# A hybrid decoder step: layer 0's input brought in row-major and channel-major, with no transposes

## The chip, the cores and the metric

The kernel runs on one core of a Trainium2 chip. The core has five engines that run side by side and meet at semaphores: TensorE (matrix products, written to PSUM), VectorE, ScalarE, GpSimd and SyncE, which here only issues DMAs. The metric is the device time of one execution in microseconds; a kernel's time is the median of its runs.

## The reference

One inference step of a decoder of two layers. Each layer adds to the residual `h` what four mixers (HGRN2, gated DeltaNet, Mamba-2 SSD, retention) make of one input projection of the normed residual:

```python
def rms_norm(x, w):                      # over the 1024 channels of a row
    x = x * lax.rsqrt(jnp.mean(x * x, axis=-1, keepdims=True) + EPS)
    return x * w
...
for l in range(DEPTH):                   # DEPTH = 2
    dp, sp = mixer(rms_norm(hp, norm_w[l]), pos_p, *lw, *zero_states(bsz), True)
    hp = hp + dp                         # prompt: 16 meta tokens + 2048 tokens, 1024 channels
    ds, ss = mixer(rms_norm(hs, norm_w[l]), pos_s, *lw, *past, False)
    hs = hs + ds                         # 8 sample tokens
```

Inside `mixer`, `proj = hn @ w_in_l` has 1024 x 4108 weights. Everything is float32.

## The kernel before

**Tiles and blocks.** The tokens are 17 tiles: tile 0 holds 16 empty rows, the 16 meta tokens and the 8 sample tokens (40 rows), tiles 1 to 16 hold 128 prompt tokens each. They form eight blocks of two tiles, the first of three. For each layer the kernel goes over all blocks in passes, one per mixer: C (SSD), B (DeltaNet), A (HGRN2), D (retention), then the output projection. The weights of a pass stay in SBUF while the blocks go by.

**The normed input.** The dense products need the normed input with the channels on the partitions, as 8 groups of 128 channels by the tokens, and split in two float32r parts: `xh` (rounded) and `xl` (the rest); three products `xh·wh`, `xl·wh`, `xh·wl` make one of nearly float32 accuracy (L484 to L486 and L494 to L497). In layer 0, `prep0` (L1701) makes it in SBUF for a block and stores it to DRAM too (L1708); passes B, A and D load it from there (`load_x`, L474). `prep0` calls `xprep` (L507) with `keep`. For a tile, `xprep` works on the token rows `hx`: ScalarE sums the squares (L358), GpSimd makes the power -1/2 (L340, L336), VectorE scales rows by it and by the norm weights, which lie in `sq128` spread over all partitions, in two halves of 512 channels (L514); TensorE transposes eight squares of 128 x 128 into two PSUM banks (L519); ScalarE rounds each bank into `xh` (L524), VectorE subtracts into `xl` (L525). In layer 1 the input comes from the output projection and goes through the same `xprep` without `keep`.

**Order.** In pass C of layer 0 `nextx(blocks[b.i + 1])` stands ahead of `mixC(L, W, b)`: the input of the next block is prepared while this block is computed. A planner orders the instructions of each engine by program order, with priorities, against a simulated timeline; engines run their lists in order. At the start the first block's input, the eight weight pieces of pass C (`wpiece`, L438: load, ScalarE's rounding L458, GpSimd's subtraction L459) and the constants come in together. Row tiles, weight pieces and some others share the pool `f4`: five buffers of 128 x 1024 float32 (L222). TensorE's dense results go to two PSUM banks (`pd`), transposes and small products to two others (`tr`). Nearly all DMAs are issued by SyncE's queue, in order.

Of the kernel before, what the change touches and what calls it, by code (L numbers as in the profile page):

```python
# [19 lines left out]
D = 1024  # L20
# [13 lines left out]
def make_consts(nch):  # L34
    f = np.float32
    jl = np.arange(32, dtype=f) * f(1 / 31)
    inv = (1 / (10000.0 ** jl.astype(np.float64)).astype(f)).astype(f)
    pos = np.zeros((nch + 1, 128), f)
    pos[0, 16:32] = np.arange(16)
    pos[0, 32:40] = PAST  # L40
    for c in range(nch):
        pos[c + 1] = 16 + 128 * c + np.arange(128)
    ang = (pos[:, :, None] * inv).astype(f).astype(np.float64)
    cs, sn = np.cos(ang).astype(f), np.sin(ang).astype(f)
    rope = np.concatenate([cs, sn], axis=-1).transpose(1, 0, 2).reshape(128, -1)
    g = np.log1p(-np.exp2(-5.0 - np.arange(4)))
    retdec = np.zeros((2, 128, 8), np.float64)
    for n, L in ((0, 32), (1, 128)):
        i = np.arange(L)[:, None]
        retdec[n, :L, :4] = np.exp(g * (i + 1))  # L50
        retdec[n, :L, 4:] = np.exp(g * (L - 1 - i)) / 8
    retdec[0, 32:40, :4] = 1
    retdec[0, 32:40, 4:] = 1 / 8
    p = np.arange(128)
    blk = p // 32
    i32 = np.arange(32)
    parts = {}
    j = (p % 32)[:, None]
    parts["hm0"] = j == i32
    parts["hm1"] = (j % 2 == 0) & (i32 == j + 1)  # L60
    for h in (2, 8):

        far = np.where(j // (4 * h) == i32 // (4 * h), i32 // h - j // h, 0)
        parts[f"hm{h}"] = np.concatenate([(far == d)[:, i32 // h % 4 >= d - (d == 1)] for d in (1, 2, 3)], axis=1)
    same = blk[:, None] == blk
    parts["l32s"] = same & (p[:, None] > p)
    parts["u32b"] = same & (p[:, None] <= p)
    parts["u32c"] = (p % 32)[:, None] <= i32
    parts["u128"] = p[:, None] <= p
    parts["hsame"] = (p // 64)[:, None] == p // 64  # L70
    rm = np.zeros((128, 4, 128))
    rm0 = np.zeros((128, 4, 32))
    for h in range(4):
        rm[:, h] = (p[:, None] <= p) * np.exp(-128 * g[h])
        rm0[:32, h] = (i32[:, None] <= i32) * np.exp(-32 * g[h])
    gg = np.stack([g[2 * pp + p // 64] for pp in range(2)], 1)
    parts["retgl"] = np.exp(128 * gg)
    parts["retg1"] = np.exp(gg)
    parts["retd0"] = retdec[0]
    parts["retd1"] = retdec[1]  # L80
    off, arrs, n = {}, [], 0
    for k, v in parts.items():
        off[k] = (n, n + v.shape[1])
        n += v.shape[1]
        arrs.append(v.astype(f))
    return rope[:, 64:], np.concatenate([rm.reshape(128, 512), rm0.reshape(128, 128), rope[:, 0:64],
                                           p[:, None] > p], axis=1).astype(f), np.concatenate(arrs, axis=1), off


class Seg:  # L90
# [3 lines left out]
def body(tc, ctx, a, o, nch, depth, blks, off):  # L94
# [268 lines left out]
    def load_layer(l):  # L363
        L = Seg()
        L.l = l
        for q in range(2):
            nc.sync.dma_start(sq128[q].rearrange("t h i -> t (h i)"),
                              a["norm_w"][l][512 * q:512 * q + 512].partition_broadcast(128))
        yield L
        pv = lp.tile([128, 10], F32, tag="pv", name="pv")  # L370
        for i, nm in enumerate(("hgrn_norm_w", "gdn_norm_w", "ssd_norm_w", "ret_norm_w", "ret_norm_b")):
# [132 lines left out]
            with early():  # L504
                evict(t, r)

    def xprep(L, t, hx, keep=False):  # L507

        b = next(x for x in blocks if t in x.tiles)
        R, x0 = rows(t), b.col[t]  # L510
        sc = rms_scale(hx, R)
        for q in range(2):
            hq = hx[0:R, 512 * q:512 * q + 512]
            stt(hq, hq, sc, sq128[q][0:R].rearrange("t h i -> t (h i)"), ALU.mult, ALU.mult)  # L514
        for q in range(2):
            ps = ptile(ptr, "tr")
            pv = ps.rearrange("p (d c) -> p d c", d=4)
            for d in range(4):
                T.transpose(pv[:, d, 0:R], hx[0:R, 512 * q + 128 * d:512 * q + 128 * d + 128], ident[0:R, 0:R])  # L519
            if keep:  # L520
                th, tl = (x[:, 4 * q:4 * q + 4, x0:x0 + R] for x in (b.xh, b.xl))
            else:
                th, tl = w2([128, 4, 128], "xth", F32R)[:, :, 0:R], w2([128, 4, 128], "xtl", F32R)[:, :, 0:R]
            S.copy(th, pv[:, :, 0:R])  # L524
            tt(tl, pv[:, :, 0:R], f32(th), ALU.subtract)  # L525
            for dst, src in () if keep else ((xhd, th), (xld, tl)):
                nc.sync.dma_start(f32(dst[b.i][:, 4 * q:4 * q + 4, x0:x0 + R]), f32(src))

    def silu2(ps, out, n):
# [1169 lines left out]


    def prep0(L, b):  # L1701
        b.xh, b.xl = xpair(b.i % 2, BW if b.i % 2 == 0 else 256)
        for t in b.tiles:
            hx = f4([128, D], "hx")
            load_h(0, t, hx)
            xprep(L, t, hx, True)
        for dst, src in ((xhd, b.xh), (xld, b.xl)):
            nc.sync.dma_start(f32(dst[b.i][:, :, :]), f32(src[:, :, 0:b.n]))  # L1708

# [115 lines left out]
def trace(nc, inputs):  # L1825
# [1 line left out]
    depth, nch = inputs["w_in"].shape[0], inputs["x_prompt"].shape[1] // 128  # L1827
    rope, retm, tab, off = make_consts(nch)
    arrays, a = {}, {}
    named = [(n, inputs[n]) for n in _INS] + [("c_rope", rope), ("c_retm", retm), ("c_tab", tab)]  # L1830
    for n, x in named:
        x = np.ascontiguousarray(x)
        arrays[f"in_{n}_dram"] = x
# [23 lines left out]
```

## Time and profile before

| | us |
|---|---|
| median of 3 runs | 2852.36 |
| lowest, highest | 2849.44, 2856.09 |
| the profiled execution | 2860.07 |
| its span in the trace | 2858.1 |
| TensorE busy in the span | 2702.7 |
| VectorE busy | 1712.1 |
| ScalarE busy | 1038.7 |
| GpSimd busy | 1066.1 |

The profile is one execution. PE is TensorE's products, PEld its weight loads, DVE is VectorE, ACT ScalarE, POOL GpSimd, SPq SyncE's queue. Products overlap in the pipeline, so that the time from one start to the next is shorter than the duration of one. In the rows, `L519 PE MATMUL tr<-ident,hx` is line 519, engine, operation, what is written and from what; `<-` behind a number names what ended an idle time.

### The profile page before, as it was taken

Reading aid. Unit: us, or ns where it says so; the run is one execution under the profiler, and the core shown is the slowest. Engines: PE = TensorE matmul, PEld = TensorE weight load, DVE = VectorE, ACT = ScalarE, POOL = GpSimd, SP = SyncE. Lnnn points to the kernel's source line nnn. Section 1 sums busy time; section 2 is a strip of 40 time slices with the busy share of each in tenths; the row PEclk is TensorE's granted clock in tenths of the full one; section 3 lists DMA queues with packets and bytes.
Section 4 is the critical chain, followed back from the end, with each engine's and each line's share of the span. In section 5 each row is a group of like instructions: output and inputs, shape, how many; then the busy total and the mean of one; then the engine's idle time right before and its main releaser. Section 6 shows DMA issues by size and latency. Waiting matters only on the chain.

```text
span 2858.1 us, 64542 instructions
## 1 busy us (share of the span) xinstructions
PE 2702.7 (95%) x25300; PEld 2461.8 (86%) x25300; DVE 1712.1 (60%) x4872; ACT 1038.7 (36%) x2621; POOL 1066.1 (37%) x2032
## 2 busy tenths in 40 slices
PE   6989999989999899999988999999999999999998
PEld 6889898889889789888878999989888887888887
DVE  5677765657656655464445767756676666445533
ACT  4445532333434422232243445223334443222321
POOL 4453546468323221210032535556673322212100
PEclk9999999999999999999999999999999999999999
DMA  7243455463321423236772423544632223331443
GB/s 177 69 139 106 148 136 146 130 175 103 108 74 61 149 77 113 77 99 212 224 227 80 127 104 115 154 121 140 181 106 72 76 89 109 99 102 67 145 140 111
DMA packets 385143, 349.16 MB, mean 122 GB/s; under 512 B 144312, under 2 KB 349616, under 8 KB 374600
## 3 DMA queue, kind: packets, MB, share of 16 engines
q1 hardware_dynamic: 381320, 335.95, 38.7%
q0 software_dynamic: 3520, 9.09, 1.6%
q8 instruction: 200, 3.28, 0.5%
q14 instruction: 103, 0.84, 0.1%
HBM read 247.05 MB, written 98.10 MB: 121 GB/s over the span
## 4 chain that ended last, share of the span: by engine, by line
PE 76%; DVE 8%; DMA 6%; ACT 3%; POOL 3%; issue 2%; SPq 1%; POOLq 0%; ACTq 0%; DVEq 0%
PE pd L494 10%; PE pd L495 9%; PE pd L497 9%; PE pd L484 9%; PE pd L485 9%; PE pd L486 9%; PE tr L236 7%; PE wo L236 4%; PE sc L236 4%; PE o L236 3%; DMA wr<-in_w_in_dram 3%; PE tr L623 1%; ACT wh L458 1%; PE tr L519 1%; DMA bld<-qkv 1%
## 5 line engine op out<-in xcount | busy, mean ns | idle before, releaser
L484 PE MATMUL pd<-xh,wh 128*128 128x256 f32 (+1 forms) x2816 | 826.9, 294 | 36.9 <-ACT wh L458 11.6
L485 PE MATMUL pd<-xl,wh 128*128 128x256 f32 (+1 forms) x2816 | 817.6, 290 | 0.0
L486 PE MATMUL pd<-xh,wl 128*128 128x256 f32 (+1 forms) x2816 | 813.2, 289 | 1.2 <-DVE wl L459 0.7
L484 PEld LDWEIGHTS pd<-xh,wh 128*128 128x128 f32 x2816 | 542.5, 193 | 58.1 <-issue 15.0
L494 PE MATMUL pd<-wh,xh 128*128 128x512 f32 (+5 forms) x1632 | 563.8, 346 | 8.1 <-DVE sraw L1409 5.1
L495 PE MATMUL pd<-wl,xh 128*128 128x512 f32 (+5 forms) x1632 | 560.0, 343 | 3.8 <-POOL wl L459 3.8
L485 PEld LDWEIGHTS pd<-xl,wh 128*128 128x128 f32 x2816 | 542.1, 193 | 5.5 <-issue 2.7
L486 PEld LDWEIGHTS pd<-xh,wl 128*128 128x128 f32 x2816 | 542.5, 193 | 4.5 <-issue 1.7
L497 PE MATMUL pd<-wh,xl 128*128 128x512 f32 (+4 forms) x1600 | 544.6, 340 | 0.0
L494 PEld LDWEIGHTS pd<-wh,xh 128*128 128x128 f32 (+1 forms) x1632 | 307.1, 188 | 44.8 <-issue 5.5
L495 PEld LDWEIGHTS pd<-wl,xh 128*128 128x128 f32 (+1 forms) x1632 | 307.4, 188 | 38.8 <-POOL wl L459 4.2
L497 PEld LDWEIGHTS pd<-wh,xl 128*128 128x128 f32 (+1 forms) x1600 | 299.8, 187 | 34.7 <-issue 2.0
L313 DVE TENSOR_TENSOR sbd<-low,tr 64x128 f32<-64x128 f32 x384 | 108.9, 284 | 122.0 <-PE tr L236 110.5
L336 POOL TENSOR_TENSOR fm<-fm,expo 128x4 f32<-128x4 f32 (+3 forms) x136 | 133.0, 978 | 85.4 <-DVE fm L614 78.0
L612 POOL TENSOR_SCALAR fm<-fm 128x4 f32<-128x4 f32 (+3 forms) x102 | 22.1, 216 | 363.2 <-DVE fm L609 335.8
L1683 DVE TENSOR_TENSOR hx<-hx,pd 128x512 f32<-128x512 f32 (+1 forms) x72 | 49.5, 687 | 153.1 <-PE pd L497 148.0
L340 POOL TENSOR_SCALAR rm<-rm 128x1 f32<-128x1 f32 (+1 forms) x51 | 14.1, 277 | 337.6 <-ACT junk L358 336.7
L244 POOL COPY bwi<-wz 32x256 f32<-32x256 f32 x128 | 58.7, 458 | 197.9 <-DVE wz L1267 195.6
L1171 POOL TENSOR_TENSOR bR<-bR,bW 128x120 f32<-128x120 f32 (+14 forms) x300 | 118.5, 395 | 20.3
L532 ACT ACTIVATE th<-pd 128x256 f32<-128x256 f32 (+2 forms) x162 | 62.6, 386 | 174.4 <-PE pd L486 130.3
L1170 POOL TENSOR_TENSOR bW<-bU,bR 128x120 f32<-128x120 f32 (+14 forms) x300 | 114.0, 380 | 29.8 <-DMA bR<-bscr 9.5
L458 ACT CAST wh<-wr 128x1024 fp32r<-128x1024 f32 x80 | 83.1, 1044 | 89.1 <-DMA wr<-in_w_in_dram 67.3
(524 smaller groups left out, 5055.7 us busy)
## 6 DMA issues: line engine op xcount, KB each, us to landing
xh<-xh SPq DMA_DIRECT2D x56, 1024.0 KB
xl<-xl SPq DMA_DIRECT2D x56, 1024.0 KB
wr<-in_w_in_dram SPq DMA_DIRECT2D x64, 512.0 KB
hx<-in_x_prompt_dram SPq DMA_DIRECT2D x32, 512.0 KB
y<-y SPq DMA_DIRECT2D x128, 128.0 KB
yf<-y SPq DMA_DIRECT2D x32, 512.0 KB
bld<-qkv SPq DMA_DIRECT2D x32, 384.0 KB
xh<-xh SPq DMA_DIRECT2D x8, 1184.0 KB
```

Of the source, the lines that this page charges most:

```text
L236: T.matmul(out, l, r, start=start, stop=stop, skip_group_check=True)
L313: tt(new[rr, :, hh], low[rr, :, hh], pv, ALU.add)
L336: G.tensor_tensor(dst, src, e.broadcast_to(list(src.shape)), ALU.pow)
L458: S.copy(hv[:, :, c0:c1], r)
L484: T.matmul(ps, hi[:, d], b.xh[:, d, 0:b.n], start=(d == 0), stop=False)
L485: T.matmul(ps, hi[:, d], b.xl[:, d, 0:b.n], start=False, stop=False)
L486: T.matmul(ps, lo[:, d], b.xh[:, d, 0:b.n], start=False, stop=(d == 7))
L494: T.matmul(ps[0:R, 0:n], xh[:, d], hi, start=(d == 0), stop=False)
L495: T.matmul(ps[0:R, 0:n], xh[:, d], lo, start=False, stop=xl is None and d == 7)
L497: T.matmul(ps[0:R, 0:n], xl[:, d], hi, start=False, stop=(d == 7))
L1170: f(wv, bcm(U_[0:2 * nu, j, j + 1:32], 1, m), bcl(R_[0:2 * nu, 0:m, j], 31 - j), ALU.mult)
L1171: f(R_[0:2 * nu, 0:m, j + 1:32], R_[0:2 * nu, 0:m, j + 1:32], wv, ALU.subtract)
```

## The change

Only layer 0 changes. The host hands in the same input a second time, as `c_xt`, with the channels on the partitions: for each tile 8 groups of 128 channels, side by side. `prep0` loads both forms of a tile, `hx` and `xt`, both from the pool `f4`. The rows serve only the sum of squares. One float32 product of the column `sc` (1/rms of each token, read 128 times over) with the identity puts the 1/rms of all tokens on every partition, in PSUM. VectorE then scales each of the eight channel groups in one operation by the norm weight, now a value per partition (`L.nw`, one load of 1024 single elements in place of the two broadcast loads of L367), and by that PSUM tile. ScalarE rounds all 1024 columns into `xh` at once, VectorE subtracts into `xl` at once, both from SBUF.

```diff
+def channel_major(inputs, nch):
+    f = np.float32
+    t0 = np.concatenate([np.zeros((16, D), f), inputs["meta_tokens"], inputs["x_sample"][:, 0]], axis=0)
+    tiles = [t0] + [inputs["x_prompt"][0, 128 * c:128 * c + 128] for c in range(nch)]
+    return np.concatenate([x.T.reshape(8, 128, len(x)).transpose(1, 0, 2).reshape(128, -1) for x in tiles], axis=1).astype(f)
...
-        for q in range(2):
-            nc.sync.dma_start(sq128[q].rearrange("t h i -> t (h i)"),
-                              a["norm_w"][l][512 * q:512 * q + 512].partition_broadcast(128))
+        if l == 0:
+            L.nw = lp.tile([128, 8], F32, tag="nw", name="nw")
+            nc.sync.dma_start(L.nw, a["norm_w"][l].rearrange("(d p) -> p d", p=128), allow_slow_non_contiguous=True)
+        else:
+            for q in range(2):
+                nc.sync.dma_start(sq128[q].rearrange("t h i -> t (h i)"),
+                                  a["norm_w"][l][512 * q:512 * q + 512].partition_broadcast(128))
...
         for t in b.tiles:
-            hx = f4([128, D], "hx")
+            R, x0 = rows(t), b.col[t]
+            hx, xt = f4([128, D], "hx"), f4([128, D], "hxt")
             load_h(0, t, hx)
-            xprep(L, t, hx, True)
+            o_ = 8 * (TR0 + 128 * (t - 1)) if t else 0
+            xt = xt[:, 0:8 * R]
+            nc.sync.dma_start(xt, a["c_xt"][:, o_:o_ + 8 * R])
+            sc = rms_scale(hx, R)
+            ps = ptile(ptr, "tr")
+            mm(ps[:, 0:R], sc.broadcast_to([R, 128]), ident[0:R, 0:R], True, True)
+            xv = xt.rearrange("p (d c) -> p d c", d=8)
+            for d in range(8):
+                stt(xv[:, d], xv[:, d], L.nw[:, d:d + 1], ps[:, 0:R], ALU.mult, ALU.mult)
+            th, tl = b.xh[:, :, x0:x0 + R], b.xl[:, :, x0:x0 + R]
+            S.copy(th, xv)
+            tt(tl, xv, f32(th), ALU.subtract)
```

`xprep` loses its argument `keep` and serves layer 1 alone.

## Rows read from the trace of the kernel before

**Rows 1.** The page: span, busy time by engine, chain that ended last
```profile
span 2858.1 us, 64542 instructions
...
PE 2702.7 (95%) x25300; PEld 2461.8 (86%) x25300; DVE 1712.1 (60%) x4872; ACT 1038.7 (36%) x2621; POOL 1066.1 (37%) x2032
...
PE 76%; DVE 8%; DMA 6%; ACT 3%; POOL 3%; issue 2%; SPq 1%; POOLq 0%; ACTq 0%; DVEq 0%
```

**Rows 2.** Stretches: us, busy PE PEld DVE ACT POOL, PEclk, DMA share, GB/s
```profile
0.00:40.00 40.00, 19.86 (x113) 18.30 (x114) 14.57 (x32) 16.79 (x27) 27.63 (x35) 0.96 0.89 222
40.00:330.00 290.00, 269.83 (x2099) 255.03 (x2098) 208.66 (x594) 152.48 (x384) 129.63 (x180) 0.97 0.39 119
```

**Rows 3.** Groups by shape, 0 to 330 us: | busy us, mean ns | idle before
```profile
L519 PE MATMUL tr<-ident,hx 128*128 128x128 f32 x128 | 21.7, 304 | 7.1 <-DVE xl L525 7.0
L525 DVE TENSOR_TENSOR xl<-tr,xh 128x512 fp32r<-128x512 f32 x32 | 21.7, 682 | 5.5 <-ACT xh L524 5.5
...
L958 DVE SCALAR_TENSOR_TENSOR cb<-pd,cwh,cb 128x256 f32<-128x256 f32 x42 | 20.0, 477 | 3.5 <-ACT cb L954 3.1
...
L524 ACT CAST xh<-tr 128x512 fp32r<-128x512 f32 x32 | 18.4, 583 | 15.8 <-PE tr L519 15.6
...
L458 ACT CAST wh<-wr 128x1024 fp32r<-128x1024 f32 x16 | 16.6, 1043 | 7.5 <-DMA wr<-in_w_in_dram 6.0 <-PE pd L485 1.4
...
L958 DVE SCALAR_TENSOR_TENSOR cb<-u,cwh,cb 128x32 f32<-128x32 f32 x6 | 1.5, 246 | 0.0
```

**Rows 4.** TensorE's weight loads in order of time: start, us
```profile
115.53 0.54 PEld L236 LDWEIGHTS tr<-cc,cb 128*128 128x128 f32 x4
...
219.44 1.01 PEld L519 LDWEIGHTS tr<-ident,hx 128*128 128x128 f32 x8
```

**Rows 5.** Lines 514 and 459, whole span: ns min/median/max
```profile
L514 DVE SCALAR_TENSOR_TENSOR hx<-hx,rm,sq x68: 734/747/2876, 9.1 to 1493.2; 128x512 f32<-128x512 f32 x64, 40x512 f32<-40x512 f32 x4
...
L459 DVE TENSOR_TENSOR wl<-wr,wh x40: 1200/1224/1505, 607.7 to 2659.2; 128x1024 fp32r<-128x1024 f32 x40
```

**Rows 6.** TensorE's waits, 40 to 330 us: total us, times, longest
```profile
PE sc L236 <- POOL cgu L1420: 8.4, 5, 4.3
PE tr L519 <- DVE xl L525: 3.2, 5, 1.1
...
PE pd L484 <- DVE hC L960: 2.0, 4, 0.8
...
PE tr L236 <- DVE xl L525: 0.8, 1, 0.8
```

**Rows 7.** The start-up in order of time, and DMA in 40 slices of 7.5 us
```profile
GB/s 183 308 107 175 400 184 174 67 53 109 243 3 3 9 9 279 20 20 4 3 280 20 35 263 114 263 214 130 32 227 182 20 19 73 74 331 34 20 87 361
...
26.51 1.34 SPq L451 DMA_DIRECT2D wr<-in_w_in_dram  x2
...
31.24 1.04 ACT L458 CAST wh<-wr 128x1024 fp32r<-128x1024 f32 x1 [2.41 <-DMA wr<-in_w_in_dram]
32.19 0.37 ACT L532 ACTIVATE th<-pd 40x256 f32<-40x256 f32 x1
...
33.24 0.56 PE L494 MATMUL pd<-wh,xh 128*128 128x268 f32 x1 [5.10 <-DVE sraw L1409]
```

**Rows 8.** The reader of a load of single elements
```profile
28.54 0.19 DVE L385 TENSOR_SCALAR cwh<-cwt 128x48 f32<-128x48 f32 x1 [3.65 <-DMA cwt<-in_ssd_conv_w_dram]
```

**Rows 9.** TensorE after a wait, and the granted clock of that stretch
```profile
160.00:190.00 30.00, 24.77 (x180) 22.96 (x179) 23.14 (x53) 13.18 (x33) 18.64 (x24) 0.89 0.46 131
...
182.00 0.80 PE L236 MATMUL sc<-cgu,l128r 128*128 128x512 f32 x1 [4.35 <-POOL cgu L1420]
...
186.30 0.43 PE L495 MATMUL pd<-wl,xh 128*128 128x268 f32 x1
...
186.71 0.28 PE L494 MATMUL pd<-wh,xh 128*128 128x268 f32 x1
```

More of the change, by code (lines that the diff above doesn't have):

```diff
@@ L505, in dense_tm, with xprep @@
                 evict(t, r)
-    def xprep(L, t, hx, keep=False):
+    def xprep(L, t, hx):
         b = next(x for x in blocks if t in x.tiles)
@@ L519, in xprep @@
                 T.transpose(pv[:, d, 0:R], hx[0:R, 512 * q + 128 * d:512 * q + 128 * d + 128], ident[0:R, 0:R])
[L520 to L523, printed above, removed]
+            th, tl = w2([128, 4, 128], "xth", F32R)[:, :, 0:R], w2([128, 4, 128], "xtl", F32R)[:, :, 0:R]
             S.copy(th, pv[:, :, 0:R])
             tt(tl, pv[:, :, 0:R], f32(th), ALU.subtract)
-            for dst, src in () if keep else ((xhd, th), (xld, tl)):
+            for dst, src in ((xhd, th), (xld, tl)):
                 nc.sync.dma_start(f32(dst[b.i][:, 4 * q:4 * q + 4, x0:x0 + R]), f32(src))
@@ L1829, in trace @@
     arrays, a = {}, {}
-    named = [(n, inputs[n]) for n in _INS] + [("c_rope", rope), ("c_retm", retm), ("c_tab", tab)]
+    named = [(n, inputs[n]) for n in _INS] + [("c_rope", rope), ("c_retm", retm), ("c_tab", tab),
+                                                ("c_xt", channel_major(inputs, nch))]
     for n, x in named:
```

## The prediction

> **What bounds the kernel now.** I read the page first, its busy shares and its chain of waits: TensorE is busy 95% of the span, and 76% of the chain that ended last is TensorE work, with VectorE next at 8% [rows 1]. So a microsecond counts if TensorE gets it back. The change touches only the first pass of layer 0 (mixer C over eight blocks, with the input preparation of the next block woven in), so next I cut that stage out by stretches. In the first 40 us TensorE is busy for half of the time: that is a start-up that waits for data. From 40 to 330 us it is busy 269.8 of 290 us (93%), VectorE 208.7 (72%), ScalarE 152.5 and GpSimd 129.6 [rows 2]. TensorE is the bound there and VectorE the runner-up. Then came the groups of the stage by shape, for prices [rows 3], the order of weight loads for TensorE's real cost [rows 4], and the list of what TensorE waited for between 40 and 330 us: mostly GpSimd's masked tiles (8.4 us), a little VectorE [rows 6]. The start-up I read last, engine by engine [rows 7].
>
> **What leaves TensorE.** 16 full tiles had eight transposes each, 128 in all [rows 3]. Eight of them run back to back in 1.01 us, 0.126 each [rows 4]. The first three tiles lie in the start-up, where TensorE is not the bound; I count tiles 3 to 16: 14 x 8 x 0.126 = 14.1 us. The replacement is one float32 product per tile, 128 x 128 by 128 columns, and the trace has such products in mixer C: they are issued as two halves each, and four halves take 0.54 us [rows 4], 0.27 a product, 14 x 0.27 = 3.8 us. Net: 10.3 us less on the engine that sets the end.
>
> **Waits that leave with them.** Transposes stopped for a PSUM bank that VectorE's subtraction still read: 3.2 us before L519, and 0.8 us before another matmul behind the same subtraction, from 40 us on [rows 6]. The new kernel takes one bank per tile instead of two, and its subtraction reads SBUF. I count 4.0 us gained; the bounds are 0 (the new product finds its bank held by eight small operations instead) and 4.0.
>
> **What VectorE gets.** Before, a tile cost two scalings of 128x512 and two subtractions of 128x512. I price the scalings at 0.75 us each (the median; a few take up to 2.88 [rows 5]) and the subtractions at 0.68 [rows 3]: 2.86 us. After: eight scalar-tensor-tensor operations of 128x128 with one operand in PSUM. The same operation takes 0.477 us at 256 elements and 0.246 at 32 [rows 3], so 0.00103 us an element and 0.213 fixed: 0.345 at 128, 2.76 for eight. The subtraction of 128x1024 from SBUF has its like in the weight split: 1.22 us [rows 5]. Sum 3.98, so 1.12 us more a tile, 14 x 1.12 = 15.7 us more of VectorE in a stage where it had 81 us free [rows 2]. Between nothing (it fills gaps) and all 15.7 I take a third, 5 us: it is nearer to nothing, since TensorE waited little for VectorE's evictions (2.0 us for the saved tail of the convolution, the next of its waits after the transposes') [rows 6], but VectorE would go from 72% to some 80%, and behind its eight operations in order stand the evictions that give TensorE its two dense banks back.
>
> Scaling in eight short pieces instead of two long ones is what the Trainium skill advises against: the page "VectorE: DVE Perf Modes", section "The TRN2 errata — SBUF-src ops pay a fixed extra latency per instruction", says that each instruction pays its latency once however short it is, and to keep tiles at 512 elements or more. Its formulas (58 cycles plus the elements for SBUF, 120 for PSUM, at 0.96 GHz) would make the eight pieces an estimated 2.07 us and the two 1.19; with that 0.74 us more a tile instead of 1.12, a third would be 3.5 us instead of 5, and the forecast 2844. The trace's fixed part, 0.213 us, is larger than the Trainium skill's 0.125, and the trace is what I use.
>
> **ScalarE, GpSimd, DMA.** ScalarE's two copies of 0.58 us from PSUM become one of 128x1024 from SBUF, which the weight split does in 1.04 us [rows 3]: 0.1 us less a tile, off the path, taken as nothing because VectorE's and TensorE's work covers it; if that cover went it would still be a gain. GpSimd's two operations a tile stay. SyncE's queue gets 17 more loads, 0.67 us of issue each if they cost what the two weight loads at 26.51 do [rows 7], some 11 us over 300, in a queue behind which stand the output stores and the stores of the prepared tiles, which nobody reads before the next pass. I cost them at nothing after the start; if a load has to wait for one of the five shared buffers, the stores behind it are late, and they have a pass of slack. The 8.4 MB over 300 us are 28 GB/s beside 119 at a DMA share of 0.39 [rows 2].
>
> **The start-up.** Here lies the larger uncertainty. The two broadcast loads of the norm weights (0.52 MB) go; one load in 1024 pieces of 4 bytes comes, and it is first in the queue. The nearest row is that of the convolution weights, several loads of 768 such pieces, whose reader at 28.54 waited 3.65 us for them [rows 8]. So some 4 to 6 us; the load is needed only after the first tile's load, sum of squares and power, and costs nothing by itself. The channel-major tiles of the first block are 1.21 MB more (296 rows of 4 KB). Net 0.69 MB more ahead of the weights, at 308 GB/s in the second 7.5 us [rows 7] 2.2 us. On the other side the row tile is free after the sum of squares instead of after its transposes, so weight pieces find a buffer sooner. Now TensorE stops for 5.10 us until 33.24: ScalarE has the eviction that would free its bank queued behind a weight piece that waits for its load, issued only at 26.51 when a buffer came free [rows 7]. Bounds: the stop goes (-5.1), or fourteen tiles instead of eleven in five buffers push the last two weight loads back by a tile's preparation each, (3.98 + 1.04) x 2 = +10. I take +2, the bytes.
>
> **The sum.** -10.3 - 4.0 + 5 + 2 = -7.3 us. The profiled execution took 2860.07 us (span 2858.1 and 2.0 around it [rows 1]); that makes 2852.8. The median of the runs shown, 2852.36, is 7.7 below the profiled one, so the forecast for a median is 2845.1, say 2845 (-0.26%). The runs of the kernel before scatter by 0.1% to either side, and 0.2% (5.7 us) is about what can be told from no change.
>
> **Rivals.** (1) VectorE swallows the gain. If about 12 of its 15.7 us reach TensorE: -10.3 - 4.0 + 12 + 2 = -0.3, 2852. For it: 72% busy, in order, two dense banks only; against it: the short waits for VectorE in [rows 6]. (2) VectorE becomes late and the clock makes it worse; this one ends slower. A wait of 4.35 us at 182 us is followed by 268-column matmuls of 0.43 us, where 0.28 is normal, until about 186.5: 4.5 us at the lower of the two clock levels, half of which is lost; the granted clock over 160 to 190 is 0.89 [rows 9]. So a wait can cost half as much again. All 15.7 us on the path, with that, are 23.6: -14.3 + 23.6 + 2 = +11, 2863. It decides once VectorE costs TensorE more than 18.0 us (14.3 - 2 + 5.7). [...] (3) The start-up starves: +10 instead of +2 gives +0.7, 2853. For it: five shared buffers; against it: the earlier release of row tiles. (4) The start-up gains as well: the 5.10 us stop goes and VectorE's work stays hidden: -14.3 - 5.1 = -19.4, 2833. That the change doesn't do what it says I leave out: the transposes of that layer are gone from the code.
>
> **How the numbers follow.** Forecast 0.45 (its own range 2838 to 2850), rival 1 0.24, rival 2 0.12, rival 3 0.10, rival 4 0.09. The range for 8 in 10 leaves out most of rival 4 and the far half of rival 2: 2835 to 2861. Faster by over 0.2%: 0.38 from the forecast and 0.09 from rival 4, 0.47. Slower by over 0.2%: rival 2 and 0.05 from rivals 1 and 3 going beyond their price, 0.17. The same: 0.36.
>
> **What would show it.** In the changed kernel's first 330 us: no transposes of row tiles, and 17 products in two halves, some 0.27 us together; eight VectorE operations a tile of about 0.35 us and one subtraction of 1.2; VectorE's busy share from 40 to 320 us near 80%; TensorE's waits for VectorE up by about 5 us beside the 4.0 that left; the first block's dense work (now restarted at 33.24 us) within 3 us of its old place; the matmuls of the next pass beginning some 8 us earlier, and that lead kept to the end. The prediction is wrong if the short operations cost 0.25 us or 0.45 instead of 0.35, if the weight pieces come later by more than 5 us, or if the instruction order, which a planner works out anew for the whole program, loses or gains in stages that the change doesn't touch.

## The result: slower

The changed kernel took 2878.57 us (median of four runs; 2876.95 without the longest), the kernel before on the same chip 2851.36: a ratio of 1.0084, 95% interval [1.0065, 1.0103], some 24 us slower. One of the four runs took 3735.68 us and is left out of the ratio. The forecast was 2845, the upper end of the range 2861. The direction is that of rival 2; its price, 2863, is 16 us short.

The page of the changed kernel, the lines that answer to [rows 1]; its profiled execution took 2880.2 us:

```profile
span 2878.5 us, 64449 instructions
...
PE 2712.9 (94%) x25198; PEld 2468.8 (86%) x25198; DVE 1728.1 (60%) x4957; ACT 1037.3 (36%) x2604; POOL 1056.0 (37%) x2032
...
PE 74%; DVE 10%; DMA 6%; POOL 3%; ACT 3%; issue 2%; SPq 1%; POOLq 0%; ACTq 0%; DVEq 0%
```

TensorE lost 102 instructions and is busy 10.2 us longer: less work took more time. The stretches of [rows 2] tell where:

```profile
0.00:40.00 40.00, 17.43 (x96) 15.52 (x97) 17.69 (x47) 15.06 (x25) 21.90 (x35) 0.96 0.88 228
40.00:330.00 290.00, 256.94 (x1868) 244.57 (x1867) 205.46 (x634) 140.67 (x341) 112.16 (x165) 0.90 0.44 137
```

From 40 to 330 us TensorE is busy 256.9 us instead of 269.8, so it stands idle 12.9 us more, and its granted clock is 0.90 instead of 0.97. One level is half the other, so 0.10 below full speed is 58 of 290 us at 1.2 GHz, where before it was 17: half of the 41 us between, some 20 us, is work lost to the clock, more than what the stops took. VectorE's busy share did not rise (71%, [rows 2] 72%): the changed kernel runs late, and by 330 us it has done less of the pass.

To see where the delay arises I matched TensorE's instructions of the two profiled runs by line, tile and order, and took the median difference of their starts over some 20 us. The changed kernel is 3.4 us behind at 95 us, 15.5 at 345 (the end of layer 0's first pass), 10.7 at 1850, 22 after 2045, 20.4 at the end. So 12.1 of the us arose between 95 and 345 us, where 12 of the 17 tiles are prepared. Nearly as much, 10.8 us, arose between 1950 us (11.2 behind) and 2045 (22.0), in a pass of layer 1 that the change does not touch and where the planner's instruction order differs. Two of TensorE's waits there, in the kernel before (1930 to 2040 us) and in the changed one (1941 to 2062):

```profile
PE tr L1215 <- DMA bld<-qkv: 2.7, 1, 2.7
PE pd L484 <- ACT wh L458: 1.6, 1, 1.6
...
PE tr L1224 <- DMA bld<-qkv: 6.0, 1, 6.0
PE pd L496 <- ACT wh L470: 4.9, 1, 4.9
```

The granted clock in the four quarters of 1941 to 2061 us is 0.89, 1.00, 0.94 and 0.95, where in the kernel before it is 1.00 in all four from 1930 to 2050. One profiled run stands up to 12 us off its kernel's median, so whole-run verdicts below rest on the timed rounds, and the matched delay serves to find places.

Groups by shape, 0 to 330 us, of the changed kernel, as in [rows 3]:

```profile
L1725 DVE SCALAR_TENSOR_TENSOR hxt<-hxt,nw,tr 128x128 f32<-128x128 f32 x128 | 35.0, 341 | 2.9 <-PE tr L244 2.8
L1728 DVE TENSOR_TENSOR xl<-hxt,xh 128x1024 fp32r<-128x1024 f32 x16 | 22.3, 1391 | 0.0
L1727 ACT CAST xh<-hxt 128x1024 fp32r<-128x1024 f32 x16 | 16.7, 1046 | 20.4 <-DVE hxt L1725 20.4
L244 PE MATMUL tr<-ident,rm 128*128 128x128 f32 x32 | 7.9, 340 | 5.3 <-POOL rm L344 3.2 <-ACT cdc L1452 2.0
```

The prices were near: 0.341 us a scaling (0.345 forecast), 1.39 a subtraction (1.22), and TensorE has 32 short halves of a product where 128 transposes were. What TensorE waited for, 40 to 330 us, as in [rows 6]:

```profile
PE pd L496 <- DVE hC L969: 10.5, 2, 5.9
PE pd L496 <- ACT u L955: 8.3, 3, 3.4
PE sc L244 <- POOL cgu L1429: 6.3, 6, 4.0
PE tr L244 <- DVE hxt L1725: 2.9, 3, 1.2
```

The wait for VectorE's saved tail of the convolution, 2.0 us in four short pieces before, is 10.5 us in two long ones. The wait for ScalarE's eviction `u` is new among the large ones. What VectorE did before the second long stop:

```profile
300.88 4.22 DVE L1725 SCALAR_TENSOR_TENSOR hxt<-hxt,nw,tr 128x128 f32<-128x128 f32 x16
305.02 0.16 DVE L958 COPY pd<-hC 128x3 f32<-128x3 f32 x1
305.08 0.41 DVE L625 TENSOR_TENSOR on<-coi,fm 128x256 f32<-128x256 f32 x1
305.41 1.22 DVE L1728 TENSOR_TENSOR xl<-hxt,xh 128x1024 fp32r<-128x1024 f32 x1
306.55 0.16 DVE L958 COPY pd<-hC 128x3 f32<-128x3 f32 x1
306.62 0.18 DVE L597 COPY eg<-tr 128x32 f32<-128x32 f32 x1
306.71 1.22 DVE L1728 TENSOR_TENSOR xl<-hxt,xh 128x1024 fp32r<-128x1024 f32 x1
```

The sixteen scalings of a block's two tiles run as one lump, and the two subtractions follow: from 300.9 to 307.9 VectorE does hardly anything but preparation. The kernel before had some 5.4 us of such work for a block, but in pieces, with the convolution's operations (L958) and saved tails (hC) between them:

```profile
281.21 0.15 DVE L960 COPY hC<-pd 128x3 f32<-128x3 f32 x1
281.28 1.93 DVE L514 SCALAR_TENSOR_TENSOR hx<-hx,rm,sq 128x512 f32<-128x512 f32 x2
283.12 0.41 DVE L1479 TENSOR_TENSOR SC<-clow,tr 128x256 f32<-128x256 f32 x1
283.45 0.47 DVE L958 SCALAR_TENSOR_TENSOR cb<-pd,cwh,cb 128x256 f32<-128x256 f32 x1
283.85 1.40 DVE L514 SCALAR_TENSOR_TENSOR hx<-hx,rm,sq 128x512 f32<-128x512 f32 x2
...
286.23 0.15 DVE L960 COPY hC<-pd 128x3 f32<-128x3 f32 x1
286.30 0.15 DVE L949 COPY pd<-hC 128x3 f32<-128x3 f32 x1
286.36 0.41 DVE L1494 TENSOR_TENSOR coi<-coi,wo 128x256 f32<-128x256 f32 x1
286.69 1.28 DVE L525 TENSOR_TENSOR xl<-tr,xh 128x512 fp32r<-128x512 f32 x2
```

And TensorE behind the lump in the changed kernel:

```profile
310.18 0.55 PE L496 MATMUL pd<-xh,wh 128*128 128x256 f32 x1 [4.55 <-DVE hC L969]
310.53 0.41 PE L497 MATMUL pd<-xl,wh 128*128 128x256 f32 x1
```

It stands 4.55 us for the bank that VectorE frees late, and its 256-column products then take 0.41 us where 0.28 is normal, as in [rows 9]. The other long stop, 5.95 us at 224, has sixteen scalings ahead of it too, in pieces of three, five, seven and one between the convolution's operations, and again the two subtractions behind them.

Short stops have slow stretches with them as well. Products that need a `tr` bank which the scalings still read stop three times, 2.9 us in all, and one of the three is this:

```profile
272.70 0.60 PE L244 MATMUL tr<-g,cst 128*128 128x8 f32 x2 [1.19 <-DVE hxt L1725]
...
277.12 0.43 PE L506 MATMUL pd<-wh,xh 128*128 128x268 f32 x1
```

From 272.7 to 279.5 us the granted clock is 0.50, and so it is for 6.8 us from the other two of these stops, 0.86 us at 109 and 0.89 us at 146. Three of the six half-clock stretches between 95 and 345 us begin there. That the short stops cause them is not shown: in the kernel before one of 1.31 us, at 143, passes without such a stretch.

### The profile page after: what moved, and what is told of

Same layout as the page of the kernel before. It is cut to its first block, busy times and chain, and to the rows that moved or that the text cites. A ratio compares the mean times of both kernels' runs of the same rounds, so it can differ in the third digit from the quotient of the medians.

```text
span 2878.5 us, 64449 instructions
## 1 busy us (share of the span) xinstructions
PE 2712.9 (94%) x25198; PEld 2468.8 (86%) x25198; DVE 1728.1 (60%) x4957; ACT 1037.3 (36%) x2604; POOL 1056.0 (37%) x2032
## 4 chain that ended last, share of the span: by engine, by line
PE 74%; DVE 10%; DMA 6%; POOL 3%; ACT 3%; issue 2%; SPq 1%; POOLq 0%; ACTq 0%; DVEq 0%
PE pd L506 10%; PE pd L507 9%; PE pd L509 9%; PE pd L496 9%; PE pd L497 8%; PE pd L498 8%; PE tr L244 7%; PE wo L244 4%; PE sc L244 4%; DMA wr<-in_w_in_dram 3%; PE o L244 3%; PE tr L632 1%; DVE hxt L1725 1%; DVE bqk L967 1%; ACT wh L470 1%
## 5 line engine op out<-in xcount | busy, mean ns | idle before, releaser
L497 PEld LDWEIGHTS pd<-xl,wh 128*128 128x128 f32 x2816 | 548.2, 195 | 6.5 <-issue 3.6
L621 POOL TENSOR_SCALAR fm<-fm 128x4 f32<-128x4 f32 (+3 forms) x102 | 23.8, 233 | 353.6 <-DVE fm L618 332.2
L348 POOL TENSOR_SCALAR rm<-rm 128x1 f32<-128x1 f32 (+1 forms) x51 | 11.7, 229 | 340.8 <-ACT junk L366 339.8
L1179 POOL TENSOR_TENSOR bW<-bU,bR 128x120 f32<-128x120 f32 (+14 forms) x300 | 115.1, 384 | 30.9 <-DMA bR<-bscr 10.6
L471 POOL TENSOR_TENSOR wl<-wr,wh 128x1024 fp32r<-128x1024 f32 x40 | 98.5, 2472 | 57.5 <-ACT wh L470 57.4
```

Of the source, the lines that this page charges most:

```text
L471: (gtt if on_pool else tt)(lv[:, :, c0:c1], r, f32(hv[:, :, c0:c1]), ALU.subtract)
L497: T.matmul(ps, hi[:, d], b.xl[:, d, 0:b.n], start=False, stop=False)
L1179: f(wv, bcm(U_[0:2 * nu, j, j + 1:32], 1, m), bcl(R_[0:2 * nu, 0:m, j], 31 - j), ALU.mult)
```

## The experiments

The theory after these rows: the lump of scalings makes TensorE's banks late, and the clock adds to it. The rivals: the new loads and their shared buffers do it; the planner's new order does it; and, whichever does, that TensorE's saved time was worth something or nothing. Beside each run: its median, the ratio to the kernel before on the same chip with its interval, and what its profiled run lost (+) or gained against the profiled run of before between 95 and 345 us, by the matching above; the last column is the same between 1950 and 2045 us, in layer 1.

| run | median us | ratio [95%] | 95 to 345 us | 1950 to 2045 us |
|---|---|---|---|---|
| the change | 2878.57 | 1.0084 [1.0065, 1.0103] | +12.1 | +10.8 |
| e1, one scaling | 2857.79 | 1.0010 [0.9990, 1.0030] | -4.2 | +0.6 |
| e2, weight on GpSimd | 2882.1 | 1.0105 [1.0082, 1.0128] | +10.1 | +11.3 |
| e3, own buffers | 2870.57 | 1.0059 [1.0042, 1.0076] | +3.0 | +10.3 |
| e4, before, null edit | 2856.81 | 1.0008 [0.9990, 1.0026] | -1.8 | +1.9 |
| e5, two long products | 2906.02 | 1.0177 [1.0127, 1.0228] | +17.5 | +10.8 |
| e6, sixteen scalings | 2886.63 | 1.0104 [1.0066, 1.0143] | +23.8 | -0.4 |
| e7, preparation behind the mixer | 2956.35 | 1.0357 [1.0313, 1.0401] | +80 | +9.6 |
| e8, change, null edit | 2873.46 | 1.0064 [1.0043, 1.0086] | +8.9 | +11.1 |
| e9, before, transposes twice | 2872.66 | 1.0073 [1.0047, 1.0098] | +8.8 | +0.1 |
| e10, before, subtractions twice | 2887.91 | 1.0117 [1.0086, 1.0148] | +18.0 | +2.8 |
| e11, change with transposes | 2877.31 | 1.0089 [1.0054, 1.0123] | +7.8 | +7.5 |
| e12, weight on ScalarE | 2894.56 | 1.0136 [1.0106, 1.0165] | +5.3 | +12.7 |
| e13, before, fewer transposes | 2866.24 | 1.0039 [1.0024, 1.0054] | +2.8 | +3.0 |
| e14, before, fewer scalings | 2851.53 | 0.9987 [0.9967, 1.0008] | -5.7 | +9.9 |
| e15, before, fewer of both | 2859.35 | 1.0021 [1.0003, 1.0040] | -6.5 | +2.2 |
| e16, one scaling, transposes | 2849.58 | 0.9984 [0.9968, 1.0001] | -2.8 | +7.9 |
| e17, four scalings | 2869.76 | 1.0046 [1.0032, 1.0061] | +6.4 | +11.4 |
| e18, one scaling, own buffers | 2844.95 | 0.9962 [0.9949, 0.9974] | -8.0 | -1.0 |

**VectorE's scalings (e1, e6, e17).** One product by 1/rms in place of the eight scalings; the norm weight is left out:

```diff
-            for d in range(8):
-                stt(xv[:, d], xv[:, d], L.nw[:, d:d + 1], ps[:, 0:R], ALU.mult, ALU.mult)
+            tt(xv, xv, bcm(ps[:, 0:R], 1, 8), ALU.mult)
```

> The changed kernel with the eight scalings of a tile replaced by one VectorE product of 128x1024 with the 1/rms tile; the norm weight of layer 0 is left out, so the output is another. VectorE's order holds two long operations a tile instead of nine. If the runs of short scalings in front of TensorE's evictions make the loss (theory A), pass C of layer 0 has stops of under 2 us, its half-clock time falls from 61 us to some 25, and the kernel takes 2840 to 2855 us. If the five shared buffers make it (theory B), it stays at 2868 to 2880. If any new order by the planner costs that much (theory C), it lies anywhere from 2845 to 2885, and the stages after pass C move too.

The time falls back to that of the kernel before. Not all of the 21 us are the price of the scalings: e1 lacks the loss near 2000 us. Between 95 and 345 us it takes 16.3 us less than the change. Its two largest waits and its stretch, 40 to 330 us:

```profile
PE pd L496 <- ACT u L955: 8.6, 4, 3.6
PE pd L496 <- DVE hC L969: 7.8, 3, 5.7
...
40.00:330.00 290.00, 262.69 (x1983) 246.94 (x1981) 207.03 (x566) 153.03 (x367) 131.00 (x179) 0.95 0.47 145
```

One of the long stops stays: 5.68 us at 218, with only 2.34 us of products and the two subtractions ahead of it. So a lump of scalings is not needed for it. What went is the other long stop (1.38 us is left at 293), the short ones for the bank that the scalings read, and more than half of the half-clock time: TensorE is idle 5.8 us less than in the change, and a clock of 0.95 instead of 0.90 is worth 14.5 of 290 us.

Sixteen scalings of 64 columns, the other way (e6):

```diff
-            for d in range(8):
+            for d in range(16):
+                k = slice(d % 2 * R // 2, d % 2 * R // 2 + R // 2)
-                stt(xv[:, d], xv[:, d], L.nw[:, d:d + 1], ps[:, 0:R], ...
+                stt(xv[:, d // 2, k], xv[:, d // 2, k], L.nw[:, d // 2:d // 2 + 1], ps[:, k], ...
```

> The changed kernel with each scaling cut in two of 64 columns: sixteen short operations a tile, the same numbers computed. By the spacing in the trace 0.26 us at 128 columns and some 0.20 at 64, so 1.0 us a tile and 17 us in all more for VectorE. Theories A1 and A2: slower than the changed kernel, 2885 to 2905 us, with more stops before the evictions of the convolution in pass C. If VectorE's scalings are not the cause: 2870 to 2885, as the changed kernel.

Its waits, 40 to 330 us:

```profile
PE pd L496 <- DVE hC L969: 13.6, 2, 7.1
PE pd L496 <- ACT u L955: 12.1, 4, 5.3
PE tr L244 <- DVE hxt L1726: 6.8, 6, 2.6
PE pd L509 <- DVE xl L1729: 6.5, 3, 2.9
```

The same stops, longer. Sixteen scalings of a tile take 3.15 us where the eight take 2.11, so 12.5 us more over 12 tiles, and the stretch takes 11.7 us more than in the change. The medians differ by 8 us only, because e6 lacks the loss near 2000 us. Only four of the eight scalings, the loads and buffers as in the change (e17; half of each tile keeps its raw values):

```diff
-            for d in range(8):
+            for d in range(4):
```

> The changed kernel with only four of the eight scalings per tile (the other half of each tile keeps its raw values): VectorE about 2.2 us a tile instead of 3.25, the new loads, the shared buffers, the product and TensorE's work as in the changed kernel. Theory A (in the steady part of the first pass, from 95 to 345 us, the delay is about 12.5 us for each microsecond of VectorE per tile above 2.65): that stretch takes 4 to 7 us less than in the kernel before, 16 to 19 less than in the changed one; the whole run about 2855. Theory B (the new loads and the shared buffers cause the loss): the stretch stays 5 to 12 us longer than before; the whole run 2868 or more.

The number that theory A forecast failed: the stretch took 5.7 us less than in the change, not 16 to 19, and the run came out where theory B had it. By medians the four kernels still stand in order, 2857.8, 2869.8, 2878.6 and 2886.6 for one, four, eight and sixteen operations a tile, but e17 and the change have some 11 us near 2000 us that e1 and e6 lack: at 1950 us the profiled e17 is 0.3 us behind the kernel before and e1 1.7 ahead. In the stretch from 95 to 345 us the order is the same (-4.2, +6.4, +12.1, +23.8). There e17 stands 10.6 us behind e1 with as much work on VectorE, which it makes up later. So the scalings cost, but not by VectorE's time per tile alone.

**The buffers (e3, e18).** The channel-major tiles get two buffers of their own (a zero tile and the norm weights' old place, which the pass does not need; the zero tile is cleared after the pass instead of before). e3 does this to the change, e18 to e1:

```diff
-            hx, xt = f4([128, D], "hx"), f4([128, D], "hxt")
+            hx = f4([128, D], "hx")
+            xt = wz.rearrange("p a b -> p (a b)") if t % 2 else sqb.rearrange("p q h i -> p (q h i)")
```

> The changed kernel with the channel-major tiles in memory of their own (the norm-weight squares and the zero-padded tile of pass B, both idle in pass C, in turn), so that the five shared buffers serve row tiles and weight pieces as before the change. Theory A: the eight scalings remain, 2868 to 2880 us. Theory B: the waits for row tiles at 57 us and at the start go and the kernel comes to 2855 or below. Theory C: anywhere from 2845 to 2885.

> One product by 1/rms in place of eight scalings (norm weight left out), and two buffers of their own for the channel-major tiles. Theory A (VectorE's time per tile is what counts): the stretch from 95 to 345 us as in the run with one scaling, 2 to 6 us shorter than before, and a whole run of 2850 to 2858. Theory B (the shared buffers eat the gain of TensorE's shorter work): 2838 to 2847.

e3 is 8 us below the change and e18 12.8 below e1; e18 falls into theory B's range and is the only kernel of the study that is measurably faster than before, without the norm weight. Two changes by two give a square of ratios: 1.0084 (eight scalings, shared buffers), 1.0059 (eight, own), 1.0010 (one, shared), 0.9962 (one, own). Along the scalings the square differs by 0.74 and 0.97%, 21 and 28 us, but the two kernels with eight scalings have the loss near 2000 us and the two with one lack it; between 95 and 345 us it is 16.3 and 11.0 us. The buffers are worth 0.25 and 0.48%, 7 to 14 us, of which 9.1 and 3.8 lie between 95 and 345 us. How shared buffers reach TensorE shows at the start of the pass, in ScalarE's timeline of the change:

```profile
57.80 1.06 ACT L366 ACTIVATE junk<-hx 128x1024 bf16<-128x1024 f32 x1 [5.20 <-DMA hx<-in_x_prompt_dram]
...
59.28 0.38 ACT L955 COPY u<-pd 128x256 f32<-128x256 f32 x1
```

The sum of squares waits 5.20 us for its row tile, and the eviction `u` stands behind it, for which TensorE stops. With shared buffers and one scaling (e1) TensorE still waits 8.6 us for `u`; with own buffers (e18) the line shrinks:

```profile
PE pd L494 <- ACT u L953: 1.9, 2, 1.1
```

That is some 7 us of stops. Own buffers cost something at the start instead: TensorE stops 7.19 us until 41.90 us for VectorE's `sraw`, where in e1 it stops 2.54 us until 31.54. The profiled e18 draws ahead of the profiled e1 mostly after the pass, though, so by which way all 12.8 us come is not settled.

**TensorE's transposes put back (e11, e16).** To the change, and to e1, eight transposes per tile that nobody reads:

```diff
+            for q in range(2):
+                pt = ptile(ptr, "tr")
+                for d in range(4):
+                    T.transpose(pt[0:R, 128 * d:128 * d + 128], xv[:, 4 * q + d], ident)
```

> The changed kernel, with eight transposes of the scaled tile into two banks that nobody reads put back per tile: some 17 us of TensorE. Theory A: 12 to 20 us later than the changed kernel, about 2893. Theory B (the changed kernel's first pass runs at VectorE's pace): within 5 us of the changed kernel, 2870 to 2882.

> The changed kernel with one product by 1/rms in place of eight scalings (norm weight left out), and eight transpositions per tile that nobody reads put back: TensorE +17 us against the run with one scaling. If that version ran at VectorE's pace, within 4 us of it (2855 to 2861); if TensorE bounds it, 12 to 20 us later (about 2873).

Some 17 us of TensorE work cost nothing: e11 takes what the change takes, e16 no more than e1. The stretches from 40 to 330 us of e11:

```profile
40.00:330.00 290.00, 264.46 (x2024) 250.00 (x2023) 205.38 (x643) 143.67 (x352) 115.83 (x171) 0.95 0.46 140
```

TensorE does 156 instructions more than the change in the same 290 us, and its granted clock is 0.95 instead of 0.90. Its stops are others too: the two long ones for `hC` are gone, one of 5.0 us for another tile has come, and the short ones for a bank that scalings read are 1.1 us in all instead of 2.9. Whether the transposes filled empty time, or their new order of instructions spared stops, is not told apart.

**TensorE and VectorE priced in the kernel before (e9, e10, e13, e14, e15).** Each transpose, or each subtraction, twice; then one transpose in place of four (the tiles get copies of it), or only the first half of each row scaled (the second keeps its raw values), or both cuts:

```diff
-            for d in range(4):
+            for d in (0, 1, 2, 3) * (2 if keep else 1):      # e9
-            tt(tl, pv[:, :, 0:R], f32(th), ALU.subtract)
+            for _ in range(2 if keep else 1):                # e10
+                tt(tl, pv[:, :, 0:R], f32(th), ALU.subtract)
-            for d in range(4):
+            for d in range(1 if keep else 4):                # e13, e15
+            pv = bcm(pv[:, 0, 0:R], 1, 4) if keep else pv
-        for q in range(2):
+        for q in range(1 if keep else 2):                    # e14, e15
```

> The kernel before, with each transposition of the row tiles in layer 0 done twice: some 17 x 8 x 0.126 = 17 us more on TensorE, nothing else moved. Theory A (TensorE has little to spare in the first pass, so what the change took from it was worth its price there): the end is 12 to 20 us later, about 2867. Theory B (VectorE, in order, sets the pace of that pass; TensorE's saved 10 to 14 us were never worth anything): 0 to 5 us later, about 2855.

> The kernel before, with each subtraction of 128x512 in layer 0 done twice: some 17 x 2 x 0.65 = 22 us more on VectorE, in long instructions from PSUM, with no buffer and no load changed. Theory A (VectorE's time in front of the convolution's evictions reaches TensorE nearly one for one, whatever the instructions are): 15 to 30 us later, about 2875. Theory B (the loss of the change is due to the new load, the shared buffers or the eight short instructions, and VectorE had room for 22 us): 0 to 7 us later, about 2855.

> The kernel before, with one transposition in place of four in layer 0 (the other three column blocks are filled with copies of the first, so the tiles hold wrong values); ScalarE and VectorE do the same work as before. 14 x 6 x 0.126 = 10.6 us less on TensorE, what the change takes from it. Theory A (TensorE's time in that pass is worth its price by itself): 8 to 13 us faster, about 2843. Theory B (VectorE, in order, holds the pass as well; TensorE's time alone is worth little): 0 to 4 us faster, about 2852.

> The kernel before, with only the first half of each row tile scaled in layer 0 (the second half keeps its raw values): 17 x 0.75 = 12.7 us less on VectorE, TensorE's work as before. Theory A (TensorE alone bounds the pass, VectorE's work is hidden): 0 to 4 us faster, about 2852. Theory B (both hold it): 4 to 10 us faster, about 2847, since shorter work in front of the evictions shortens TensorE's stops and their slow stretches.

> Both cuts of the two runs beside it together. If the two engines hold the pass in turn, the gain is larger than the sum of the single ones: 12 to 25 us faster, about 2838. If TensorE alone bounds it, it equals the run with fewer transpositions (about 2843). If neither is worth anything, within 4 us of the kernel before.

Taken by their medians e9 and e10 meet theory A, and e13 is absurd: less work, more time. The trace shows why the medians mislead here. All five profiled runs are 11 to 14 us behind by 95 us (e13, e14 and e15 make most of it up by the end); in e9, e10 and e13 most of it is one wait. TensorE's first line of waits in e9, 40 to 330 us:

```profile
PE sc L236 <- POOL cgu L1420: 19.4, 5, 13.7
```

GpSimd, which makes `cgu`, stood before a product with the decode step's state, and SyncE issued that state's load behind six small loads (e9):

```profile
60.69 12.57 SPq L1359 DMA_DIRECT2D dgb<-smd  x6
73.42 2.23 SPq L1534 DMA_DIRECT2D dcS<-in_state_ssd_dram  x1
...
86.68 1.90 POOL L1537 TENSOR_TENSOR dcS<-dcS,dce 128x1024 f32<-128x1024 f32 x1 [32.65 <-issue]
```

In the kernel before the load goes out 11.6 us earlier, ahead of most of them:

```profile
61.79 3.00 SPq L1534 DMA_DIRECT2D dcS<-in_state_ssd_dram  x1
64.83 6.95 SPq L1359 DMA_DIRECT2D dgb<-smd  x1
...
73.83 1.91 POOL L1537 TENSOR_TENSOR dcS<-dcS,dce 128x1024 f32<-128x1024 f32 x1 [19.43 <-DMA dcS<-in_state_ssd_dram]
```

So the edit moved a load in SyncE's order, and that wait says nothing of the price of a transpose. Only the stretch behind it does (12 tiles). There, e9's 12 us more of TensorE (12 x 1.01) cost 8.8; e10's 16 us more of VectorE (24 x 0.68) cost 18.0; e13's 9.1 us less of TensorE (12 x 6 x 0.126) gained nothing, +2.8; e14's 9 us less of VectorE (12 x 0.75) gained 5.7; and e15, both cuts, 6.5, not more than e14 alone. More TensorE costs nearly its price, less of it gives nothing; VectorE pays both ways. These are single profiled runs, good to a few us.

**Where else the weight can be multiplied (e2, e5, e12).** In place of the eight scalings, one product with 1/rms on VectorE, and the norm weight on GpSimd, on VectorE in one long operation, or on ScalarE:

```diff
+            gtt(xv, xv, bcl(L.nw, R), ALU.mult)              # e2
+            tt(xv, xv, bcl(L.nw, R), ALU.mult)               # e5
+                S.mul(xv[:, d], xv[:, d], L.nw[:, d:d + 1])  # e12, for each d
+            tt(xv, xv, bcm(ps[:, 0:R], 1, 8), ALU.mult)      # all three
```

> The changed kernel with the norm weight applied by GpSimd, one product of 128x1024 a tile before the 1/rms is known, and one VectorE product for the 1/rms. VectorE as in the run with one scaling, GpSimd 17 x 2.4 = 41 us more. Theory A: 2842 to 2858 us, a little above the run with one scaling where GpSimd's masked tiles come later. Theory B: 2868 to 2882, since the tile is held longer. Theory C: anywhere from 2845 to 2885.

> The changed kernel with two long VectorE products a tile in place of the eight short ones: 128x1024 by the norm weight (it needs no 1/rms and can run early), then 128x1024 by the 1/rms tile. VectorE has about as much work a tile as with the eight (3 x 1.2 = 3.6 us with the subtraction, against 8 x 0.26 + 1.2 = 3.3 by the spacing in the trace). If VectorE's total time a tile is what costs (theory A1), the kernel stays at 2865 to 2885 us, as the changed kernel. If it is the number of short operations and how the planner lines them up in front of the evictions (theory A2), it comes back to 2848 to 2862, as with one scaling.

> The changed kernel with the norm weight multiplied by ScalarE (eight multiplications of 128x128 per tile), and 1/rms by one VectorE product of 128x1024: the same output, VectorE down to about 2.3 us a tile, ScalarE up by about 8 x 0.3 = 2.4 us a tile. Theory A (VectorE's place in front of the evictions is what costs, and ScalarE has room for 40 us in this pass): 2845 to 2860. Theory B (ScalarE evicts for TensorE as well, so the wait only moves to it): 2865 to 2885.

None is faster than the change. In e2 the wait moves: TensorE waits for GpSimd's `cgu` 7.6 us and `css` 6.4. In e12 TensorE stops 18.4 us for ScalarE's `u` in one piece, but ScalarE stands for a load there, as in e9:

```profile
61.17 12.57 SPq L1368 DMA_DIRECT2D dgb<-smd  x7
73.84 2.62 SPq L1719 DMA_DIRECT2D hxt<-in_c_xt_dram  x1
...
87.37 2.44 ACT L1725 ACTIVATE hxt<-hxt,nw 128x128 f32<-128x128 f32 x8 [18.24 <-DMA hxt<-in_c_xt_dram]
```

Between 95 and 345 us e12 loses 5.3 us, less than the change, so its median does not say that ScalarE has no room. In e5 TensorE stops 15.2 us for `u` in one piece, and VectorE, whose weight product needs only the new load and so stands early in its order, waits for that load for 31.9 us in all; e5 therefore says little about long against short operations.

**Order (e4, e8, e7).** A memset of two columns per tile on VectorE makes the planner work out its order anew; e7 issues the next block's preparation behind the mixer of this one:

```diff
+            V.memset(k2.tile([128, 2], F32, tag="nul", name="nul"), 0.0)   # e4 on before, e8 on the change
-            if not b.last:
+            if not b.last and l:                                           # e7
                 nextx(blocks[b.i + 1])
             mixC(L, W, b)
+            if not b.last and not l:
+                nextx(blocks[b.i + 1])
```

> The kernel before with one more VectorE operation a tile in layer 0's preparation, a memset of two columns of some 0.07 us that nobody reads: 17 x 0.07 = 1.2 us of VectorE. It asks what a new order alone does. Theories A and B: within 3 us of the kernel before, 2849 to 2856. Theory C: it moves by 6 us or more to either side, with the order changed in stages far from the memsets.

> The changed kernel with the memset of the run on the kernel before: 17 x 0.07 us of VectorE that nobody reads. It asks how much of the loss belongs to this one order. If the loss is a property of the work (A1): 2872 to 2884. If orders decide (theory C), it moves by 6 us or more, and the 11 us that the changed kernel loses in pass B of layer 1 (near 2000 us) come out otherwise.

> The changed kernel with the preparation of the next block written behind the mixer's work on this block in layer 0, so that the planner gives it the lower priority. If the loss is scalings that stand in front of evictions which TensorE waits for (theory A), the stops in pass C shrink: 2845 to 2865 us. If it is the sum of VectorE's work (A1), no change: 2865 to 2885. It could also be late for the next block: over 2885, with stops at the first dense product of each block.

The memsets are worth 2 us on the kernel before and some 5 on the change, neither measurable. They do not clear the order, though: near 2000 us they left it as it was. From 1900 to 2070 us TensorE, VectorE, ScalarE and SyncE run the order of the kernel before in e1, e4, e6, e9, e10, e13 to e16 and e18, and that of the change in e2, e3, e8, e12 and e17; e5, e7 and e11 share most of it. The kernels with the change's order lose 10.3 to 12.7 us there, e5, e7 and e11 7.5 to 10.8, those with the order of before at most 3.0, except e14 and e16, where TensorE waits 10.5 and 9.4 us for the load `bld`. So some 11 us of the change come with an order that the planner chose, in a pass that the change does not touch. e7 makes the next block wait for its tiles and loses 100 us; it was the wrong way to take the preparation out of VectorE's road.

## Why the prediction was wrong, by its own steps

**What bounds the kernel.** TensorE does set the end: its stops and its clock make the delay of the pass. But of "a microsecond counts if TensorE gets it back" the condition failed: in this pass a microsecond taken off TensorE did not come back.

**What leaves TensorE, -10.3, and the waits, -4.0.** The work left, as priced. It was worth nothing: e11 and e16 put more than it back for free, e13 took it out of the kernel before without gain in the stretch. The waits on the subtraction left, and 2.9 us for a bank that the scalings still read came in their place; the prediction had named such a wait for its lower bound.

**What VectorE gets, +5.** This is the step that failed most. Its price was on the high side: the recorded 0.341 us is a duration, and sixteen scalings follow each other in 4.22 us, 2.11 a tile and not 2.76. The Trainium skill's page "VectorE: DVE Perf Modes", section "The TRN2 errata — SBUF-src ops pay a fixed extra latency per instruction", gave an estimated 2.07 for them, and the row above agrees with it; the prediction held its own larger fixed part for the better one and was wrong there. With 1.22 for the subtraction a tile takes 3.33 us of VectorE's line, against 1.40 + 1.28 = 2.68 in the rows of before shown above: 0.65 more, 11 us over 17 tiles. A third of the added time was to reach TensorE. Over the 12 tiles from 95 to 345 us, about all of it did where it was tried: 18.0 us for 16 added (e10), 11.7 for 12.5 (e6 against the change), 16.3 and 11.0 for the 11.3 between eight scalings and one product (2.11 - 1.17 = 0.94 a tile; e1's two products of a block take 2.34), and 5.7 came back for 9 removed (e14). The prediction counted a share of busy time.

**Rival 2** had the direction, a late VectorE with the clock on top, and was given 0.12. It still counted TensorE's 14.3 us as gained and 15.7 us more on VectorE, so its sum is not what happened either. Half-clock stretches came with the stops of 4.55 and 5.95 us, and also with those of 0.9 to 1.2 us.

**ScalarE, GpSimd, DMA, 0.** Wrong by 7 to 14 us, by e3 and e18. One way is shown: the row tile that comes late to a shared buffer holds up ScalarE, and behind it stands an eviction. The prediction looked at the stores behind such a load and not at ScalarE.

**The start-up, +2.** The 3.4 us at 95 us are near it by luck. At 45 us the changed kernel is 0.2 us behind, and its first dense product restarts at 33.05 us, where before it was 33.24: the bytes cost nothing that shows. The 3.4 us come after that, with stops of 2.90 and 3.35 us for `u` at 51 and 60 us.

**The order** was named as a thing that could make the prediction wrong, and the sum had nothing for it. It is the second step that failed: 10.8 of the profiled run's 20.4 us arose near 2000 us, with an order of the planner.

In the profiled run the delay is 3.4 us by 95 us, 12.1 more by 345, 4.8 made up by 1850, some 11 more near 2000, and 20.4 at the end. For the 12.1 the terms in their new sizes are an estimate: TensorE 0, VectorE 12 x 0.65 = 8 at its full price, the buffers 4 to 9. That VectorE's 8 us count in full in the change is argued from the other runs, not measured by itself. Three things stay open: why four scalings (e17) stand 10.6 us behind one long product at 345 us although they keep VectorE no longer (2.15 us for the eight of a block, against 2.34), why the planner's order near 2000 us costs what it does, and which part of e18's 11 us ahead of the kernel before is the missing norm weight.

## What to carry to other kernels

Before taking work off the busiest engine, take some of it out in a run that leaves that part undone: if nothing comes back, as in e13, the saving will turn into a wait. Adding work there is another test: in the kernel before it cost 8.8 of 12 us (e9), although removing it gained nothing. Price work that is added to a second, in-order engine at its full time, not by the engine's share of the stage: here 0.6 to 1.4 of it reached the end of the pass. When an edit makes a planner reorder the program, look where the delay arises before reading a price from the total: 13 us of e9 were a load that moved in a queue, and 11 us of the change lie in a layer that it leaves alone.

## What the runs showed of the hardware

The spacing of short VectorE operations is less than their recorded duration: 128x128 scalings with a PSUM operand are recorded at 0.341 us and follow each other every 0.264. With unread transposes put in, TensorE's granted clock was 0.95 instead of 0.90 over the same 290 us, and the program took as long (2877.31 and 2878.57 us) with some 17 us of work more. And TensorE ran at the lower of its two clock levels for 6.8 us beside stops of 0.86, 0.89 and 1.19 us, as it did beside one of 5.95.
